# Layer 0 of a streaming encoder trunk on one core: half B's x^T through the staging pool, dense GLA products ahead of the decay products, the cache set-up queued at step 8, half B's recurrences written behind the projection

## The chip, the cores and the metric

The kernel runs on one core of a Trainium2 chip. The metric is the device time of one execution in microseconds (us), lower is better. Four compute engines work side by side, each through its own instructions in order: PE (TensorE, matmuls), DVE (VectorE), ACT (ScalarE) and POOL (GpSimd). SP (SyncE) issues nearly all DMAs, also in order; an instruction that waits on it holds up every DMA issue behind it.

## The reference, cut to what matters

Two layers over 1024 prompt frames and 64 sample frames, all float32. Layer 0 is the one that the change touches:

```python
p   = x @ w_in_mix                       # 1024 -> 3344 columns, for every frame
ya  = rwkv7_time_mix(p[..., :1792])      # mixer A: 8 heads x 64, a recurrence over time
yb  = gla_mix(p[..., 1792:])             # mixer B: 4 heads, key 64, value 128, chunked recurrence
#     q, k, v, xa, rg = split(p[..., 1792:])
#     log_a = log_sigmoid(xa @ alpha_up + alpha_bias) / 16     (the decay)
mix = concat([ya, yb]) @ w_out_mix
x   = layer_norm(alpha * x + mix)
x   = layer_norm(alpha * x + swiglu(x, w_ffn_in, w_ffn_out))
```

Layer 1 replaces the two mixers by chunk-band softmax attention, in which sample frames also read a cache of 128 earlier K and V rows per head.

## The kernel before, in words

The frames are cut into half A (384 prompt frames and the 64 sample frames, 448 columns) and half B (640 prompt frames). Every large product is done to float32 accuracy with three matmuls: each operand is split into a rounded high part and a low part (`wh`/`wl` for weights, `xh`/`xl` for x^T), and high*high, high*low and low*high are summed in one PSUM bank. `load_w` (L93) brings a 512 KB weight piece into `wr` (two buffers), casts it on ACT (L100) and takes the difference on DVE (L105) or POOL (L107); `wh` and `wl` have four buffers each. `load_xt` (L207) does the same for x^T: a DMA into a raw tile (L213), the cast to `xh` on ACT (L214), the difference `xl` on DVE or POOL (L215). Without a pool its raw tile is one of the two `wr` buffers; with the pool `yp` it is one of eight `yr` buffers. `gemm_ws` (L115, rows L123 to L125) and `gemm_ts` (L127, rows L134 to L137) are the dense products, with three PSUM banks `gps` in turn.

Half B's x^T has storage of its own for three of its eight pieces (`xeh`, `xel`); the other five lie in the storage of half A's x^T (`xt_tiles_in`, L195). The mixers' results of half A are later brought into that storage as well (`load_xt(0, self.yg_d, ...)`, from the DRAM tensor `yg_d`).

Order of layer 0 as written in `run` (L1331): input products of half A for mixer A (`inproj_rwkv`), the first four steps of its recurrences, then those for mixer B (`inproj_gla`, L338), then the rest of half A's recurrences (`rwkv`, `gla`); half B's x^T, `inproj_gla(1)` and `inproj_rwkv(1)`; half A's mixer results into x^T; `self.PRE` = 4 steps of half B's recurrences; the output projection of half A with its layer norm (`proj`, L853, wname `w_om`); the other recurrence steps of half B; the feed-forward of half A (`ffn`), whose 22 steps carry side work: at step 6 `bias_setup`, at step 8 `cache_setup` (L1111). `inproj_gla` computes first the decay (the narrow products L351 into 32 rows, the float32 products L362, then activations on DVE, ACT and POOL), then q and k (four weight pieces through `gemm_ws`), then v (L134 to L137), then the gate.

One recurrence step of mixer A is a unit that passes through `rw1` (loads rkv, xg, rsb; matmuls L436 to L438), `rw1b` (L483, L508 to L510), `rw2` (L576 to L583 and a chain of small DVE operations, L548 and L550), `rw3` (L610 to L621) and `rw4` (L648, the result goes to `yg_d` at L653). Mixer B's unit is `gla_unit` (L724 to L755, result at L759). Their matmuls are small, 64 or 128 columns each.

`cache_setup` handles four groups of V rows one after another: load `cv` (L1116, one buffer), cast to `cvh` on ACT (L112), difference on DVE (L113), write to DRAM (L1119); then two groups of K rows (L1122 to L1130).

The written order is not the order on the engines. A scheduler that runs while the kernel is built gives each engine its order: of the instructions that its own model of time has ready, the one written first goes first; a waiting one lets later ones by. So side work can be placed far ahead of where it is written. On the chip each engine then keeps that order whatever the real times are. `tc.issue_after(i)` puts every instruction that its block writes for the engine of `i` behind `i` on that engine; `last_w` is the latest weight DMA on SP.

Of the kernel before, what the change touches and what calls it, by code (L numbers as in the profile page):

```python
# [9 lines left out]
F32 = mybir.dt.float32  # L10
# [9 lines left out]
NA, NB = PA + 64, 1024 - PA  # L20
NM = max(NA, NB)
# [61 lines left out]
class Kern:  # L83
# [9 lines left out]
    def load_w(self, src, shape):  # L93

        nc = self.nc
        raw = self.wp.tile(shape, F32, tag="wr", name="wr", bufs=2)
        self.last_w = nc.sync.dma_start(raw, src).ins
        hi = self.wp.tile(shape, F32R, tag="wh", name="wh", bufs=self.WB)
        lo = self.wp.tile(shape, F32R, tag="wl", name="wl", bufs=self.WB)
        self.A.copy(hi, raw)  # L100
        self.wcount += 1
        m = shape[1]
        h = m * 5 // 8 if self.both else m * (self.wcount % 2)
        if h:
            self.V.tensor_tensor(lo[:, :h], raw[:, :h], hi[:, :h].bitcast(F32), op=ALU.subtract)  # L105
        if h < m:
            self.G.tensor_tensor(lo[:, h:], raw[:, h:], hi[:, h:].bitcast(F32), op=ALU.subtract)  # L107
        return hi, lo
# [229 lines left out]
    def inproj_gla(self, hf, pool):  # L338
        nc, V, A, G, T = self.nc, self.V, self.A, self.G, self.T
        n, c0, xt = self.N[hf], self.base[hf], self.xt[hf]  # L340

        raw = pool.tile([128, 8, 16], F32, tag="xar", name="xar", bufs=1)
        nc.sync.dma_start(raw, self.a["w_xa"])
        whl = pool.tile([128, 8, 32], F32R, tag="xaw", name="xaw", bufs=1)
        A.copy(whl[:, :, 0:16], raw)
        V.tensor_tensor(whl[:, :, 16:32], raw, whl[:, :, 0:16].bitcast(F32), op=ALU.subtract)
        segs = self.banks(hf)
        for kt in range(8):
            for i, xx in enumerate((xt.h(kt), xt.l(kt))):
                for ps, s0, w in segs:  # L350
                    T.matmul(ps[0:32, :], whl[:, kt, :], xx[:, s0 : s0 + w], start=(kt + i == 0), stop=(kt + i == 8))  # L351
        xa = pool.tile([32, NM], F32, tag="xa", name="xa", bufs=1)
        for ps, s0, w in segs:
            V.tensor_copy(xa[:, s0 : s0 + w], ps[0:32, :])
        up = pool.tile([32, 256], F32, tag="up", name="up", bufs=1)
        nc.sync.dma_start(up, self.a["up2"])
        for p in range(2):
            segs = self.banks(hf)
            mn = pool.tile([128, NM], F32, tag="sq", name="mn", bufs=3)[:, :n]
            ab = pool.tile([128, NM], F32, tag="sq", name="abz", bufs=3)[:, :n]  # L360
            for ps, s0, w in segs:
                T.matmul(ps, up[:, 128 * p : 128 * p + 128], xa[:, s0 : s0 + w], start=True, stop=True)  # L362
                V.tensor_scalar(mn[:, s0 : s0 + w], ps, self.ab[:, p : p + 1], 0.0, op0=ALU.add, op1=ALU.min)
                A.activation(ab[:, s0 : s0 + w], ps, AF.Abs, bias=self.ab[:, p : p + 1])
            A.activation(ab, ab, AF.Exp, scale=-1.0)
            A.activation(ab, ab, AF.Ln, bias=self.one)
            G.tensor_tensor(ab, ab, mn, op=ALU.subtract)
            nc.sync.dma_start(self.qkl_d[2, p, :, c0 : c0 + n], ab)
        for ct in range(4):
            w = self.load_w(self.a["w_in"][14 + ct], [128, 8, 128])  # L370
            segs = self.banks(hf)
            self.gemm_ws(w, xt, segs)
            t = pool.tile([128, NM], F32, tag="t1", name="gq", bufs=2)
            for ps, s0, wd in segs:
                A.copy(t[:, s0 : s0 + wd], ps)
            nc.sync.dma_start(self.qkl_d[ct // 2, ct % 2, :, c0 : c0 + n], t[:, :n])
        ws = []
        for i in range(4):
            hi, lo = self.load_w(self.a["w_gv"][i], [128, 2, 512])
            ws += [(hi[:, 0, :], lo[:, 0, :]), (hi[:, 1, :], lo[:, 1, :])]  # L380
        for i0 in range(0, n, 128):
            m = min(128, n - i0)
            ps = self.bank()[:m]
            self.gemm_ts(ps, ws, xt.h, xt.l, list(range(8)), lambda x: x[:, i0 : i0 + m])
            t = pool.tile([128, 512], F32, tag="xs", name="gvs", bufs=2)
            A.copy(t[:m], ps)
            nc.sync.dma_start(self.gv_d[c0 + i0 : c0 + i0 + m, :], t[:m])
        for ct in range(4):
            w = self.load_w(self.a["w_in"][18 + ct], [128, 8, 128])
            segs = self.banks(hf)  # L390
            self.gemm_ws(w, xt, segs)
            t = pool.tile([128, NM], F32, tag="t1", name="grg", bufs=2)
            for ps, s0, wd in segs:
                A.activation(t[:, s0 : s0 + wd], ps, AF.Tanh, scale=0.5)
                V.scalar_tensor_tensor(t[:, s0 : s0 + wd], t[:, s0 : s0 + wd], 1.0, ps, op0=ALU.add, op1=ALU.mult)
            nc.sync.dma_start(self.sg_d[ct, :, c0 : c0 + n], t[:, :n])
# [934 lines left out]
    def run(self):  # L1331
        nc, tc, a = self.nc, self.tc, self.a
# [2 lines left out]
        self.gla_d = self.dp.tile([2, 128, 128], F32, name="gla_d", tag="gla_d")  # L1335
        self.JX = 6
        self.PB, self.QB, self.turn, self.AQ = 1, 2, 0, (1, 4)
        self.HB, self.PRE, self.JO, self.JM = 5, 4, 16, 18
        es_scan, es_one, es_ps = ExitStack(), ExitStack(), ExitStack()
        self.sp_ps = es_ps.enter_context(tc.tile_pool(name="scps", bufs=1, space=PS))  # L1340
        self.tpsum = lambda: self.sbank("tps")
# [3 lines left out]
        yp = es_yr.enter_context(tc.tile_pool(name="yr", bufs=1))  # L1345
# [16 lines left out]
        for _ in g:  # L1362
            pass
        self.xt[1] = self.xt_tiles_in(es_one.enter_context(tc.tile_pool(name="xb", bufs=1, side="right")), 8 - NA * 8 // NB)
        self.load_xt(1)
        self.inproj_gla(1, one)
        self.inproj_rwkv(1, one)
        nc.sync.dma_start(a["s_shift"].rearrange("c p -> p c"), self.shS)
# [27 lines left out]
        for j in self.ffn(0, 0, acc0, hp, lambda: self.layer_norm(0, acc0, "ln2", 0, xd(0))):  # L1396
            if j == 6:
                self.bias_setup(hp)
            if 12 <= j < 20:
                for h in range(2 * j - 24, 2 * j - 22):  # L1400
                    self.bias_copies(h)
            if j == 8:
                with tc.tile_pool(name="as", bufs=1) as asp:
                    self.cache_setup(asp)
        for p in range(4):
            self.wkv_out(sc, S[p], a["p_wkv"][2 * p : 2 * p + 2])
# [173 lines left out]
```

## Time and profile before

| | us |
|---|---|
| Median of 3 runs (lowest to highest) | 3120.83 (3118.74 to 3125.66) |
| Profiled execution, its own time | 3122.28 |
| its span, first to last instruction | 3120.5 |
| PE busy in the span | 3010.1 |
| DVE / POOL / ACT busy | 2018.0 / 1347.8 / 1263.3 |
| mean granted PE clock | 0.977 |

"Busy" is the time in which at least one instruction of the engine ran. The granted clock is the share of TensorE's full rate; in stretches it is one half. A line of the timeline reads: start, length, engine, line, operation, output <- inputs, and in brackets the engine's idle time just before it with what ended that. A line of the stage table reads: from:to, length, then busy time (and instructions) of PE, PEld (weight loads), DVE, ACT, POOL, then granted clock, the DMA engines' busy share and GB/s. A line of the waits reads: who waited for whom, total us, times, longest.

### The profile page before, as it was taken

To read this page: it belongs to the slowest core of one execution; us is meant where nothing else is said; L and a number is where in the kernel's file an instruction comes from. 1 tells how busy PE (TensorE), PEld (TensorE's weight loads), DVE (VectorE), ACT (ScalarE), POOL (GpSimd) and SP (SyncE) were. 2 spreads that over 40 slices of the span, in tenths; PEclk is the share of its full clock that TensorE was granted. 3 is DMA by queue.
4 is the path that set the end of the run, shared out by engine and by line. 5 is a ranking of instruction groups with operands and counts; after the bars stand their busy time and mean duration, and the time that the engine had idled before them with its cause. 6 is when DMAs were issued, how large, how long until landed. Compare 5 with 4: busy or idle time off the path is not lost. (4 is left out here: it accounts for less than half of the span.)

```text
span 3120.5 us, 50008 instructions
## 1 busy us (share of the span) xinstructions
PE 3010.1 (96%) x17468; PEld 2675.3 (86%) x17468; DVE 2018.0 (65%) x4933; ACT 1263.3 (40%) x2753; POOL 1347.8 (43%) x1481
## 2 busy tenths in 40 slices
PE   8999999799999999999999999999999989899998
PEld 7888888688888887888999899899999978799987
DVE  5677875779898764375554466244666657866567
ACT  4454554344454323334442132354444433333332
POOL 2354533445455333343342233244555445754444
PEclk9989999889999999999999999999999999999999
DMA  6554434533533228534342222766445532322222
GB/s 200 141 154 120 108 111 122 141 109 107 145 106 110 85 100 277 180 98 122 116 130 97 81 95 99 240 192 190 126 139 141 150 130 82 116 84 95 63 86 75
DMA packets 297340, 395.10 MB, mean 127 GB/s; under 512 B 125376, under 2 KB 218424, under 8 KB 297088
## 3 DMA queue, kind: packets, MB, share of 16 engines
q1 hardware_dynamic: 295936, 389.28, 41.8%
q8 instruction: 138, 2.26, 0.3%
q10 hardware_dynamic: 1152, 2.62, 0.2%
q14 instruction: 114, 0.93, 0.1%
HBM read 319.44 MB, written 75.51 MB: 127 GB/s over the span
## 5 line engine op out<-in xcount | busy, mean ns | idle before, releaser
L107 POOL TENSOR_TENSOR wl<-wr,wh 128x512 fp32r<-128x512 f32 (+2 forms) x289 | 506.2, 1756 | 629.5 <-ACT wh L100 590.0
L123 PE MATMUL gps<-xh,wh 128*128 128x320 f32 (+1 forms) x2188 | 747.8, 342 | 9.0 <-ACT xh L214 5.9
L124 PE MATMUL gps<-xl,wh 128*128 128x320 f32 (+1 forms) x2188 | 746.5, 341 | 0.6 <-DVE xl L215 0.6
L125 PE MATMUL gps<-xh,wl 128*128 128x320 f32 (+1 forms) x2188 | 744.0, 340 | 0.7 <-DVE wl L105 0.6
L100 ACT CAST wh<-wr 128x1024 fp32r<-128x1024 f32 x352 | 366.9, 1048 | 468.2 <-PE gps L124 147.0
L105 DVE TENSOR_TENSOR wl<-wr,wh 128x512 fp32r<-128x512 f32 (+2 forms) x289 | 284.0, 983 | 255.1 <-ACT wh L100 253.2
L123 PEld LDWEIGHTS gps<-xh,wh 128*128 128x128 f32 x2188 | 415.5, 190 | 30.6 <-ACT xh L214 5.9
L125 PEld LDWEIGHTS gps<-xh,wl 128*128 128x128 f32 x2188 | 414.6, 189 | 19.5 <-DVE wl L105 1.8
L124 PEld LDWEIGHTS gps<-xl,wh 128*128 128x128 f32 x2188 | 414.8, 190 | 18.4 <-DVE xl L215 1.0
L1288 POOL TENSOR_SCALAR s<-s,mx 128x640 f32<-128x640 f32 (+5 forms) x144 | 203.6, 1414 | 289.6 <-DVE mx L1287 250.6
L134 PE MATMUL gps<-wh,xh 128*128 128x512 f32 x661 | 261.3, 400 | 11.5 <-ACT xh L214 7.1
L135 PE MATMUL gps<-wl,xh 128*128 128x512 f32 x661 | 261.5, 398 | 1.1 <-DVE wl L105 0.8
L137 PE MATMUL gps<-wh,xl 128*128 128x512 f32 x661 | 257.3, 397 | 4.8 <-DVE xl L215 4.8
L134 PE MATMUL gps<-wh,hh 128*128 128x512 f32 x572 | 225.9, 397 | 0.4 <-DVE acc L825 0.3
L135 PE MATMUL gps<-wl,hh 128*128 128x512 f32 x572 | 226.0, 396 | 0.0
L825 DVE TENSOR_TENSOR acc<-acc,gps 128x512 f32<-128x512 f32 (+1 forms) x216 | 143.7, 679 | 86.0 <-PE gps L137 80.7
L137 PE MATMUL gps<-wh,hl 128*128 128x512 f32 x484 | 189.8, 397 | 2.9 <-DVE hl L936 2.9
L548 DVE TENSOR_TENSOR t<-lt,x 16x48 f32<-16x48 f32 (+9 forms) x540 | 147.6, 273 | 39.9 <-DMA lt<-l_d 29.4
L1286 ACT ACTIVATE s<-s,mx 128x640 f32<-128x640 f32 (+5 forms) x144 | 96.5, 670 | 178.6 <-DVE mx L1285 172.1
L134 PEld LDWEIGHTS gps<-wh,xh 128*128 128x128 f32 x661 | 125.3, 190 | 40.9 <-ACT xh L214 7.3
L137 PEld LDWEIGHTS gps<-wh,xl 128*128 128x128 f32 x661 | 124.7, 189 | 32.4 <-DVE xl L215 5.3
L550 DVE TENSOR_TENSOR x<-x,t 16x48 f32<-16x48 f32 (+9 forms) x540 | 144.0, 267 | 10.9
(355 smaller groups left out, 6307.4 us busy)
## 6 DMA issues: line engine op xcount, KB each, us to landing
wr<-in_w_fi SPq DMA_DIRECT2D x176, 512.0 KB
wr<-in_w_fo SPq DMA_DIRECT2D x88, 512.0 KB
wr<-in_w_in SPq DMA_DIRECT2D x44, 512.0 KB
wr<-in_w_qk SPq DMA_DIRECT2D x32, 512.0 KB
qs<-qd SPq DMA_DIRECT2D x32, 320.0 KB
wr<-in_w_om SPq DMA_DIRECT2D x16, 512.0 KB
wr<-in_w_v SPq DMA_DIRECT2D x16, 512.0 KB
vd<-vh SPq DMA_DIRECT2D x16, 512.0 KB
```

What stands on the lines that cost most here:

```text
L100: self.A.copy(hi, raw)
L105: self.V.tensor_tensor(lo[:, :h], raw[:, :h], hi[:, :h].bitcast(F32), op=ALU.subtract)
L107: self.G.tensor_tensor(lo[:, h:], raw[:, h:], hi[:, h:].bitcast(F32), op=ALU.subtract)
L123: self.T.matmul(ps, hi[:, kt, :], xh, start=(kt == 0), stop=False)
L124: self.T.matmul(ps, hi[:, kt, :], xl, start=False, stop=False)
L125: self.T.matmul(ps, lo[:, kt, :], xh, start=False, stop=(kt == nk - 1))
L134: self.T.matmul(ps, xh, wh, start=(i == 0), stop=False)
L135: self.T.matmul(ps, xh, wl, start=False, stop=(lo is None and i == n - 1))
L137: self.T.matmul(ps, cols(lo(kt)), wh, start=False, stop=(i == n - 1))
L548: V.tensor_tensor(tv, lt[:, j, w:16].unsqueeze(2).to_broadcast([m, r, w]), x[:, 0, j, 0:w].unsqueeze(1).to_broadcast([m, r, w]), op=ALU.mult)
L550: V.tensor_tensor(x[:, 0, w:16, 0:w], x[:, 0, w:16, 0:w], tv, op=ALU.add)
L1288: G.tensor_scalar(s[:m, :nk], s[:m, :nk], mx[:m, 3:4], None, op0=ALU.mult)
```

## The change

Four edits, all in layer 0; no product and no element-wise operation is added or dropped.

1. Half B's x^T comes through the eight `yr` buffers instead of the two `wr` buffers, and each piece in two halves of 320 columns: sixteen loads, casts and differences instead of eight of 640 columns.
2. In `inproj_gla` the q and k products stand ahead of the decay products, for both halves.
3. `cache_setup` is written inside two `issue_after` blocks: its DMAs stand behind the latest weight DMA on SP, its ACT operations behind the latest weight cast on ACT. For that `load_w` keeps the cast as `last_cast`.
4. `self.PRE` is 0 instead of 4: no step of half B's recurrences is written ahead of the projection of half A.

```diff
@@ load_w
-        self.A.copy(hi, raw)
+        self.last_cast = self.A.copy(hi, raw).ins
@@ inproj_gla, ahead of the decay products
+        for ct in range(4):
+            w = self.load_w(self.a["w_in"][14 + ct], [128, 8, 128])
+            segs = self.banks(hf)
+            self.gemm_ws(w, xt, segs)
+            t = pool.tile([128, NM], F32, tag="t1", name="gq", bufs=2)
+            for ps, s0, wd in segs:
+                A.copy(t[:, s0 : s0 + wd], ps)
+            nc.sync.dma_start(self.qkl_d[ct // 2, ct % 2, :, c0 : c0 + n], t[:, :n])
@@ inproj_gla, behind the decay products: the same eight lines
-        for ct in range(4):
...
@@ run
-        self.HB, self.PRE, self.JO, self.JM = 5, 4, 16, 18
+        self.HB, self.PRE, self.JO, self.JM = 5, 0, 16, 18
@@ run
-        self.load_xt(1)
+        for kt in range(8):
+            for c in (0, NB // 2):
+                self.load_xt(1, None, (kt,), slice(c, c + NB // 2), yp)
@@ run, step 8 of the feed-forward of half A
-                with tc.tile_pool(name="as", bufs=1) as asp:
+                with tc.tile_pool(name="as", bufs=1) as asp, tc.issue_after(self.last_w), tc.issue_after(self.last_cast):
                     self.cache_setup(asp)
```

What the scheduler makes of it, at three places. In the changed file the lines from L341 on shift (the decay's L351 is L359, L362 is L370, L1369 is L1371).

PE, where half A's last dense product ends. Before, small products of half A's recurrences follow and then half B's decay products (`xaw` holds their weights; `xeh` and `xel` are half B's own x^T pieces):

```order
L125 MATMUL gps<-xh_69,wl 128x448
L436 MATMUL pa<-xg,w2z 128x128
L437 MATMUL pa<-xg,a2z 128x128
L438 MATMUL pa<-xg,g_209 128x128
L576 MATMUL pz<-tt,lab 128x64
L610 MATMUL ps<-sv,ro 64x64
L648 MATMUL py<-ident,on 128x64
L351 MATMUL gps<-xeh,xaw 32x320 x2
L351 MATMUL gps<-xel,xaw 32x320 x2
```

Now the same place goes on with half B's first dense product:

```order
L438 MATMUL pa<-xg,g_209 128x128
L576 MATMUL pz<-tt,lab 128x64
L614 MATMUL ps<-rr,btt 64x64 x2
L648 MATMUL py<-ident,on 128x64
L123 MATMUL gps<-xeh,wh 128x320
L124 MATMUL gps<-xel,wh 128x320
L125 MATMUL gps<-xeh,wl 128x320
```

The decay products of half B moved behind four dense weight pieces; there, ahead of half B's v products, they again stand in one block with small products and no dense one.

SP, where half B's last input product ends (`rkv_d` is its result in DRAM, `acc` the accumulator of the projection, `gb` the layer norm's weights, `yraw` a piece of half A's mixer results). Before, with loads of the cache (`cv`), of half B's first recurrence units (`rkv`) and the last `yg_d` write and `yraw` load behind them:

```order
L1116 DMA cv<-in_ck_v 128x4x64
L302 DMA rkv_d<-xs 128x640
L1369 DMA out_dram<-shP 128x14x1
L97 DMA wr<-in_w_om 128x1024
L426 DMA rkv<-rkv_d 128x3x128
L653 DMA yg_d<-y 128x128
L1119 DMA vd<-cvh 128x512
L1116 DMA cv<-in_ck_v 128x4x64
L213 DMA yraw<-yg_d 128x448
```

Now, the last `yg_d` write and the last `yraw` load standing further ahead and no cache load near:

```order
L302 DMA rkv_d<-xs 128x640
L1371 DMA out_dram<-shP 128x14x1
L866 DMA gb<-in_ln_w 128x1024
L866 DMA gb<-in_ln_b 128x1024
L796 DMA acc<-in_x 128x1024 x3
L796 DMA acc<-in_x 64x1024
L426 DMA rkv<-rkv_d 128x3x128 x2
```

The loads of `acc` and `gb` moved ahead of the load of half B's first units.

ACT, at the cache's V rows (`cvh`). Before, at the start of the projection of half A, between operations of the recurrences and ahead of the cast of a `yraw` piece:

```order
L112 CAST cvh<-cv 128x4x64
L612 COPY rr<-ps 64x128
L753 ACTIVATE gon<-gon,grstd 128x128
L112 CAST cvh<-cv 128x4x64
L440 ACTIVATE th<-pa,w0h 128x128
L442 ACTIVATE tha<-pa,a0h 128x128
L444 COPY gt<-pa 128x128
L214 CAST xh_69<-yraw 128x448
```

Now, in the feed-forward of half A, behind two weight casts:

```order
L100 CAST wh<-wr 128x1024 x2
L112 CAST cvh<-cv 128x4x64
L615 ACTIVATE uv<-ps 64x128
L716 ACTIVATE genb<-gb 128x64
L732 COPY gkt<-gpa 128x128
L493 COPY ro<-ar 64x2x128 x2
L629 COPY on<-ps 128x128
L501 COPY ec<-eb 64x2 x2
L746 COPY gon<-gps 128x128
L714 ACTIVATE geb<-gb 128x64
L112 CAST cvh<-cv 128x4x64
```

The four casts moved some 300 operations back on ACT and stand eight or more operations apart there.

More of the change, by code (lines that the diff above doesn't have):

```diff
@@ L368, in inproj_gla @@
             nc.sync.dma_start(self.qkl_d[2, p, :, c0 : c0 + n], ab)
-        for ct in range(4):
[L370 to L376, printed above, removed]
         ws = []
```

## The prediction

> **What bounds the kernel now.** I read the page first, then the stage table, then the waits, then the timelines of the stages that stood out. From the page:
>
> ```profile
> span 3120.5 us, 50008 instructions
> PE 3010.1 (96%) x17468; PEld 2675.3 (86%) x17468; DVE 2018.0 (65%) x4933; ACT 1263.3 (40%) x2753; POOL 1347.8 (43%) x1481
> ```
>
> PE is busy for 3010.1 of 3120.5 us and the change takes no matmul away. So it can win only two things: PE's idle time, 110 us in all, and the time in which PE is busy at half clock. The stage table, cut where the change acts, shows where these lie:
>
> ```profile
> 169.00:203.00 34.00, 31.65 (x153) 23.96 (x152) 25.39 (x71) 19.96 (x54) 19.84 (x36) 0.65 0.50 148
> 203.00:534.00 331.00, 325.12 (x2317) 290.06 (x2316) 252.91 (x906) 165.87 (x494) 141.08 (x264) 0.99 0.42 120
> 534.00:567.00 33.00, 18.09 (x79) 14.52 (x77) 18.78 (x65) 11.42 (x35) 11.02 (x17) 0.70 0.66 136
> 567.00:611.00 44.00, 42.37 (x220) 34.52 (x219) 39.00 (x98) 14.88 (x39) 21.27 (x26) 0.99 0.51 142
> 611.00:646.00 35.00, 27.94 (x141) 22.19 (x140) 30.68 (x80) 16.24 (x47) 23.53 (x30) 0.62 0.37 114
> 646.00:1014.00 368.00, 363.69 (x2296) 313.30 (x2295) 321.50 (x1058) 171.77 (x516) 179.87 (x290) 0.99 0.42 115
> ```
>
> Three short stages have a low clock: the passage from half A's to half B's input products (169 to 203, clock 0.65), the start of half A's output projection (534 to 567, 14.9 us idle, clock 0.70) and its layer norm (611 to 646, clock 0.62). Everything else up to 1014 us runs at 0.99. What PE waited for from 470 to 650 us:
>
> ```profile
> PE pb L483 <- ACT gt L444: 8.5, 1, 8.5
> PE gps L137 <- DVE xl L215: 4.8, 1, 4.8
> PE pz L581 <- ACT ys L579: 4.4, 1, 4.4
> ```
>
> The longest is named after an ACT copy, but ACT's timeline shows who held ACT, and SP's who held that:
>
> ```profile
> 545.88 0.40 ACT L753 ACTIVATE gon<-gon,grstd 128x128 f32<-128x128 f32 x1
> 558.62 0.40 ACT L112 CAST cvh<-cv 128x256 fp32r<-128x256 f32 x1 [12.33 <-DMA cv<-in_ck_v]
> 559.43 0.26 ACT L444 COPY gt<-pa 128x128 f32<-128x128 f32 x1
> 560.20 0.56 ACT L214 CAST xh<-yraw 128x448 fp32r<-128x448 f32 x1 [0.50 <-DMA yraw<-yg_d]
> ```
> ```profile
> 542.18 0.51 SPq L302 DMA_DIRECT2D rkv_d<-xs  x1
> 543.27 1.37 SPq L97 DMA_DIRECT2D wr<-in_w_om  x1
> 552.67 0.36 SPq L426 DMA_DIRECT2D rkv<-rkv_d  x1
> 553.12 0.44 SPq L653 DMA_DIRECT2D yg_d<-y  x1
> 554.12 0.39 SPq L1116 DMA_DIRECT2D cv<-in_ck_v  x1
> 557.57 0.32 SPq L213 DMA_DIRECT2D yraw<-yg_d  x1
> 561.45 1.82 SPq L796 DMA_DIRECT2D acc<-in_x  x4
> ```
>
> SP stood from 544.6 to 552.7 before the load of a half-B unit (L426). Behind it queued the last result of half A (L653), the cache load (L1116) and the last x^T piece (L213). ACT then stood 12.33 us before the cast of that cache load, with `gt` and everything of the projection behind it. So two pieces of work that the projection doesn't need, the cache set-up and half B's first units, hold it up. What SP waited for is in its own list:
>
> ```profile
> SPq L426 <- DMA rkv_d<-xs: 9.2, 2, 8.0
> ```
>
> **Edit by edit.** The sum is made against the profiled execution, 3122.28 us (span 3120.5, 1.8 us around it); it lies 1.45 us above the median of the runs, 3120.83.
>
> *Edits 3 and 4 at the projection.* Two marks in PE's timeline:
>
> ```profile
> 534.39 0.50 PE L134 MATMUL gps<-wh,xh 128*128 128x512 f32 x1
> 559.75 2.08 PE L483 MATMUL pb<-ar,bbk 128*128 128x128 f32 x8 [8.51 <-ACT gt L444]
> 567.06 0.80 PE L134 MATMUL gps<-wh,xpk 128*128 128x512 f32 x1
> ```
>
> Between the first and the third, 32.7 us, PE did 36 dense matmuls; at full pace they follow each other every 0.23 us:
>
> ```profile
> 574.84 0.39 PE L134 MATMUL gps<-wh,xh 128*128 128x512 f32 x1
> 575.06 0.39 PE L135 MATMUL gps<-wl,xh 128*128 128x512 f32 x1
> ```
>
> That is 8.3 us; the small products that now stand among them take about 4 us more, and the first two differences of x^T 1 to 2 us: some 14 us at best. But the row at 567.06 needs a fourth PSUM bank, so the first accumulation on DVE must be done, and that needs `acc`. In the new order the `acc` loads stand behind the `rkv_d` write and, I assume, wait for it to land, since `acc` takes over storage of the input products. From the rows: the write is issued 8 us after the dense work ended (542.18 against 534.39) and lands 10.5 us later (552.6) at most; without the cache's traffic beside it I take 5. From the issue of `acc` to the accumulation,
>
> ```profile
> 565.73 0.67 DVE L823 SCALAR_TENSOR_TENSOR acc<-acc,gps 128x512 f32<-128x512 f32 x1
> ```
>
> 4.3 us pass (561.45 to 565.73), to which the `gb` loads ahead add perhaps 3. So the third mark comes at 8 + 5 + 4.3 + 3 = 20 us, between 14 and 26, instead of 32.7: **-12 us (-19 to -6)**. The wait on `acc` is what is late next. The late `yg_d` write is no longer: it stands ahead of the last two input products' writes.
>
> *The rest of the projection and its layer norm*, 567 to 646. DVE is busy for 39.00 of 44 and 30.68 of 35 us there, nearly the bound. With edits 3 and 4 fewer recurrence and cache operations stand among the projection's on DVE (79 rows against 99 by the order, from half B's last input product to the first layer-norm operation; 73 against 85 inside the norm), which at 0.4 us each could give 8 to 13 us back. Against it, some ten more small products of the recurrences stand in PE's queue between the last dense product and the feed-forward, where the clock is 0.62; eight such matmuls took 2.08 us at 559.75, so ten items of two to four are 5 to 10 us. I take **-4 us (-10 to +5)**.
>
> *Edits 1 and 2 at the passage to half B.*
>
> ```profile
> 170.47 0.47 PE L351 MATMUL gps<-xeh,xaw 128*32 128x320 f32 x2
> 177.44 0.48 PE L351 MATMUL gps<-xl,xaw 128*32 128x320 f32 x2 [0.96 <-DVE xl L215]
> 198.31 0.64 PE L123 MATMUL gps<-xeh,wh 128*128 128x320 f32 x1
> ```
>
> For 28 us no dense product runs. The granted share of 0.65 over 34 us is 11.9 us lost to the clock, though PE hardly idles, and 2.4 us are idle: 14 us at stake. Edit 2 puts dense products right behind half A's. Edit 1 has most raw data in `yr` by then, so only casts and differences remain. They cannot start before half A's last products, since five of the eight pieces lie in half A's storage. POOL takes 0.8 us for a half piece (half of the row below), six in a row, while PE's first piece needs one every six matmuls of 320 columns, 0.9 us by the 0.23 us for 512: a stall of 0 to 3 us.
>
> ```profile
> 167.33 1.56 POOL L215 TENSOR_TENSOR xl<-xraw,xh 128x640 fp32r<-128x640 f32 x1 [3.98 <-ACT xh L214]
> ```
>
> The block of decay products isn't dissolved, it comes later, with some 14 small items among it instead of 26. If it loses as this one does, in proportion, that is about 8 us, plus 2 for the new passage: **-4 us (-11 to +2)**.
>
> Here the Trainium skill bears. "TensorE: Matmul & The Clock Gate", section "What's actually happening", says that the clock halves after an idle window of about 3.4 us and is full again after one busy window. By that, neither this block nor the layer norm's tail should stay at half clock while filled. The table disagrees: 31.65 of 34 us busy at 0.65, 27.94 of 35 at 0.62. Small products alone did not keep the clock up here, and the sum goes by the table.
>
> *Edit 1 at the start.* Sixteen issues on SP instead of eight, at 0.32 to 0.51 us by SP's rows above: 8 x 0.4 = 3.2 us more of SP, and 2.6 MB moved into half A's products, ahead of weight loads that run with buffers to spare. Hidden there by dense work; I take **+1 us (-1 to +4)**. The Trainium skill's "DMA: Bandwidth & Descriptors", "Rules for kernel authors", speaks against halving: it asks for transfers of 1 MiB or more and for coalescing. No run here shows this load's rate either way.
>
> *Edit 3 at step 8.* The four casts now queue in ACT in the feed-forward, each behind a DMA on SP, and weight casts, PSUM evacuations and recurrences queue behind them. What ACT and PE waited for from 646 us on:
>
> ```profile
> ACT btt L565 <- DMA t<-t_d: 19.9, 11, 5.5
> PE gps L137 <- DVE hl L936: 2.9, 2, 1.7
> PE tps L895 <- DVE xl L113: 2.6, 1, 2.6
> ```
>
> ACT stands before such DMAs up to 5.5 us at a time there already, and PE's two largest sums of waits up to 1170 us are 2.9 and 2.6 us. Four more of 2 to 5 us each are covered by the weights in four buffers; if that cover is gone, each costs what it exceeds. **+1 us (0 to +12)**.
>
> *All else in the new order.* From 203 to 534 and 646 to 1014 PE idles 5.9 and 4.3 us; the order there is new throughout and will have waits of its own: **+1 us (-4 to +7)**.
>
> Sum: -12 - 4 - 4 + 1 + 1 + 1 = -17 us, so 3122.3 - 17 = 3105 us.
>
> **The rivals.** *The wait moves to `acc` (no change).* If the `rkv_d` write takes its 10.5 us and `gb` delays `acc` by 4 more, the third mark is at 26 us; DVE, standing before `acc`, has the recurrences behind it and gives back nothing, and the block of decay products costs as much as before: -6 + 2 = -4, 3118 us. For it: DVE at 88% in the stage. Against it: the cache's traffic is gone from the queues.
>
> *Slower: the cache set-up stalls the feed-forward.* The 12.33 us on ACT came from SP standing before another wait, and at step 8 SP also has recurrence loads between the `cv` loads. One such stall cost PE 8.5 us and some 3 of the 9.9 us that the clock took in that stage (0.30 of 33). The first cast has its load well ahead; three could repeat it, 3 x 12 = 36 us at about 12 each, and with -17 that is +19: 3141 us. Two give +7. It decides from two stalls over 10 us on; against it, ACT's waits there end within 5.5 us.
>
> *More than forecast.* By the rule of the clock gate above, filled stretches run at full clock: of the 13.3 us that the layer norm loses to its clock and the 11.9 of the passage, the 12 that the sum leaves lost would go too: 3105 - 12 = 3093 us. The table speaks against it.
>
> *An edit does not act.* The scheduler places by readiness, so PRE = 0 need not move half B: the first L648 of half B stands at about the same place on PE in both orders. Then only the cache's stall goes: the last `yg_d` write would still stand 8 us on SP. About -9 us, 3113.
>
> **How the numbers follow.** Forecast (gain of 8 to 25 us) 0.50; the wait moves to `acc` 0.20; stalls at step 8, or other waits of the new order, slower 0.14; full clock 0.06; an edit does not act 0.10. A measurement of this kernel can tell about 0.2%, 6.2 us. Faster: 0.50 + 0.06 + 0.09 of the last = 0.65; same: 0.20 + 0.01 = 0.21; slower 0.14. The range leaves out the full-clock case below and most of the slower case above: 3090 to 3126.
>
> **What would show it.** Right: no `cvh` cast before 700 us; the mark of the first `xpk` matmul 15 to 25 us behind the projection's first, with DVE's wait before it named `acc`; a clock above 0.85 in that stage; a first half-B dense matmul within 5 us of half A's last. Wrong: that mark after 30 us; ACT waits over 10 us at `cvh` in the feed-forward with PE idle beside them; a layer norm longer than 40 us from the last dense product to the feed-forward; new PE waits over 5 us between 200 and 530 us.

## The result and the profile after

The changed kernel takes 3151.09 us (median of 4 runs, 3149.59 to 3151.56), the kernel before 3122.41 beside it: ratio 1.0093, 95% interval 1.008 to 1.0106. It is 29 us slower, where 17 us faster was forecast. From the page of the profile after:

```profile
span 3149.6 us, 50092 instructions
PE 3030.0 (96%) x17468; PEld 2685.2 (85%) x17468; DVE 2003.8 (64%) x4937; ACT 1264.1 (40%) x2761; POOL 1345.3 (43%) x1485
```

PE has the same 17468 matmuls, is busy 19.9 us longer and idles 9.2 us longer. To see where, both programs are cut at the same work, counted in PE's dense products (rows L123 to L137): after the 600th (half A's input products are nearly done), the 1000th (half B's q, k and decay are done), the 1800th (half A's projection starts), the 2000th (feed-forward), the 3400th, the 3600th (entry to the attention stage) and the 3800th. The stage table of before:

```profile
5.90:164.20 158.30, 152.42 (x719) 128.28 (x720) 95.86 (x296) 73.64 (x139) 51.82 (x58) 0.97 0.58 167
164.20:304.50 140.30, 136.33 (x833) 116.43 (x833) 106.86 (x343) 73.05 (x205) 65.69 (x114) 0.91 0.46 136
304.50:534.40 229.90, 225.64 (x1664) 202.43 (x1662) 172.29 (x635) 115.34 (x348) 97.17 (x186) 0.99 0.42 117
534.40:650.10 115.70, 92.10 (x452) 74.64 (x450) 90.78 (x253) 42.91 (x121) 57.15 (x76) 0.79 0.49 126
650.10:1132.40 482.30, 477.99 (x2949) 410.09 (x2948) 395.38 (x1229) 213.09 (x604) 216.57 (x330) 1.00 0.39 110
...
1192.60:1237.70 45.10, 44.42 (x205) 37.56 (x204) 21.32 (x27) 20.15 (x28) 20.04 (x14) 1.00 0.88 298
```

and the same stages of the changed kernel:

```profile
6.00:177.30 171.30, 158.06 (x722) 130.13 (x723) 95.11 (x299) 76.05 (x149) 54.52 (x60) 0.94 0.59 172
177.30:316.30 139.00, 138.57 (x902) 118.69 (x901) 106.32 (x391) 77.45 (x227) 74.33 (x134) 0.96 0.41 120
316.30:553.50 237.20, 225.07 (x1594) 200.03 (x1594) 169.75 (x622) 114.71 (x335) 91.55 (x173) 0.96 0.40 112
553.50:665.70 112.20, 96.64 (x463) 77.93 (x463) 87.45 (x239) 33.74 (x88) 44.25 (x59) 0.76 0.43 106
665.70:1155.20 489.50, 484.28 (x2935) 413.24 (x2934) 388.91 (x1211) 216.35 (x626) 220.97 (x343) 0.99 0.40 113
...
1215.50:1268.60 53.10, 46.80 (x204) 38.67 (x203) 22.17 (x28) 20.84 (x30) 24.18 (x18) 0.94 0.85 276
```

Stage by stage the change costs +13.0, -1.3, +7.3, -3.5 and +7.2 us, then +0.1 in the stage left out, +8.0 at the entry to the attention stage and -1.8 in all the rest: 29 us. The projection with its layer norm, for which 16 of the 17 us were forecast, gives 3.5. The loss sits at places for which the prediction had no term, or only the +1 of "all else": half A's input products, half B's behind the decay block, the feed-forward, and the entry to the attention stage, some 150 us behind the cache's last write (1063 us). A good part of it is PE's clock, the third figure from the end of each row: it falls in five of the six stages, and one minus it, times the stage's length and summed over the six rows, is 60 us against 44. Idle time has its share too: in the third stage PE idles 12.1 us (237.2 less 225.07) instead of 4.3.

The start of the projection in the changed kernel, on PE, DVE and SP (three answers of the timeline):

```profile
553.51 0.77 PE L134 MATMUL gps<-wh,xh 128*128 128x512 f32 x1
...
578.66 0.77 PE L134 MATMUL gps<-wh,xpk 128*128 128x512 f32 x1 [7.19 <-DVE x L550]
```
```profile
577.76 0.69 DVE L823 SCALAR_TENSOR_TENSOR acc<-acc,gps 128x512 f32<-128x512 f32 x1 [10.29 <-DMA acc<-in_x]
```
```profile
558.89 0.33 SPq L302 DMA_DIRECT2D rkv_d<-xs  x1
559.27 0.43 SPq L1371 DMA_DIRECT2D out_dram<-shP  x1
...
561.74 0.63 SPq L866 DMA_DIRECT2D gb<-in_ln_b  x1
572.28 1.87 SPq L796 DMA_DIRECT2D acc<-in_x  x4
```

The first `xpk` product comes 25.2 us behind the first product, and DVE waits 10.29 us for `acc`, as forecast. `acc` is late because SP stands from 562.4 to 572.28 for the `rkv_d` write to land: 13.4 us from its issue, where the prediction took 5. Between the two stands a row that the prediction passed over, in before as well: the output of the shift vectors.

### The profile page after: what moved, and what is told of

Read it like the earlier page. It is cut to its first block, busy times and chain, and to the rows that moved or that the text cites. A ratio compares the mean times of both kernels' runs of the same rounds, so it can differ in the third digit from the quotient of the medians.

```text
span 3149.6 us, 50092 instructions
## 1 busy us (share of the span) xinstructions
PE 3030.0 (96%) x17468; PEld 2685.2 (85%) x17468; DVE 2003.8 (64%) x4937; ACT 1264.1 (40%) x2761; POOL 1345.3 (43%) x1485
## 5 line engine op out<-in xcount | busy, mean ns | idle before, releaser
L123 PE MATMUL gps<-xh,wh 128*128 128x320 f32 (+1 forms) x2188 | 750.3, 343 | 12.5 <-ACT wh L100 6.5
L100 ACT CAST wh<-wr 128x1024 fp32r<-128x1024 f32 x352 | 367.0, 1048 | 482.8 <-PE gps L124 159.5
L123 PEld LDWEIGHTS gps<-xh,wh 128*128 128x128 f32 x2188 | 416.5, 190 | 35.0 <-ACT wh L100 8.1
L137 PE MATMUL gps<-wh,xl 128*128 128x512 f32 x661 | 258.2, 398 | 0.2 <-DVE xl L215 0.2
L137 PE MATMUL gps<-wh,hl 128*128 128x512 f32 x484 | 188.3, 395 | 0.0
L135 PEld LDWEIGHTS gps<-wl,xh 128*128 128x128 f32 x661 | 127.1, 192 | 32.3 <-DVE wl L105 4.1
L137 PEld LDWEIGHTS gps<-wh,xl 128*128 128x128 f32 x661 | 125.0, 189 | 28.5 <-DVE xl L215 0.9
```

What stands on the lines that cost most here:

```text
L100: self.last_cast = self.A.copy(hi, raw).ins
L123: self.T.matmul(ps, hi[:, kt, :], xh, start=(kt == 0), stop=False)
L135: self.T.matmul(ps, xh, wl, start=False, stop=(lo is None and i == n - 1))
L137: self.T.matmul(ps, cols(lo(kt)), wh, start=False, stop=(i == n - 1))
```

## The experiments

All ratios are against runs of before on the same chip, in brackets the 95% interval. Before's medians there are 3118.7 to 3121.0 us; beside the changed kernel it was 3122.4. So where a run is compared with the changed kernel, the excess of each over its own before is what counts: 28.7 us for the changed kernel.

### Each edit alone

The first question was which edit loses. The diff of each is its part of the change, on before.

*Edit 1 alone.* 

> Before with edit 1 alone (half B's x^T through the staging pool, in column halves). Theory 1, the decay products: the 19 us that the changed kernel has lost when it reaches half A's output projection come from edit 2, so this run lies within 5 us of before (ratio 0.9984 to 1.0016) and its passage to half B is shorter than before's 34 us. Theory 2, x^T: sixteen loads, casts and differences queued among half A's input products delay these; then this run alone is 10 to 20 us slower (1.003 to 1.006), lost between 100 and 180 us.

Measured: 3128.09 us, ratio 1.0025 (1.0014 to 1.0036).

*Edit 2 alone.* 

> Before with edit 2 alone (decay products behind the q and k products, both halves). Theory 1, the decay products: half A's decay block now stands where PE has only small products beside it, it stalls PE and halves its clock, and the recurrences that need its result bunch up behind it: 10 to 20 us slower (1.003 to 1.006), and half A's projection starts at 544 to 554 us instead of 534. Theory 2, x^T: within 5 us of before (0.9984 to 1.0016).

Measured: 3143.15 us, ratio 1.0071 (1.0056 to 1.0086).

*Edit 3 alone.* 

> Before with edit 3 alone (cache set-up held back to step 8). Theory A: it does what the prediction said, the stall of 8.5 us before pb and its clock loss go and nothing new comes in the feed-forward: 5 to 14 us faster (0.9955 to 0.9984). Theory B: the gain is given back in the feed-forward and behind it, where the set-up now shares ACT and SP with the recurrences: within 5 us of before (0.9984 to 1.0016).

Measured: 3131.66 us, ratio 1.0034 (1.0023 to 1.0045).

*Edit 4 alone.* 

> Before with edit 4 alone (PRE 4 to 0). Theory A: the recurrences of half B come later, in a feed-forward where DVE is already busy 321 of 368 us; their longer chain delays the feed-forward and wkv_out: 5 to 12 us slower (1.0016 to 1.004). Theory B: the projection and its layer norm gain what the feed-forward loses: within 5 us of before (0.9984 to 1.0016).

Measured: 3142.18 us, ratio 1.0068 (1.0054 to 1.0082).

Every edit alone loses, about 7, 22, 11 and 21 us: twice the loss of all four together. So the losses are not sums of separate prices. And none lies in a range set for it: edit 1 falls between its two theories, edits 2 and 4 lose more than any foresaw, and edit 3 was to win or cost nothing. Edit 3 was to remove a stall of 8.5 us; this is PE's longest wait between 525 and 700 us in its trace, and after it that of edit 4 alone:

```profile
PE pt L508 <- DVE t L548: 10.3, 1, 10.3
```
```profile
PE pb L483 <- POOL lw L450: 10.5, 1, 10.5
```

The stall is there without the cache set-up, and it is there without the early units. Neither by itself was its cause. And in three of the four traces (edits 1, 3 and 4) the stage from the 3600th to the 3800th dense product takes 51 to 53 us instead of 45.1, as in the changed kernel.

### What holds up the projection: one small output

The bytes that the DMA queues moved answer the first. In before, over 8 us behind the shift output, and in 10 us behind the other shift output (94 to 104 us, issued at 91.61 by L1368):

```profile
DMA packets 1081, 0.38 MB, mean 47 GB/s; under 512 B 986, under 2 KB 986, under 8 KB 1081
```
```profile
DMA packets 71, 0.29 MB, mean 29 GB/s; under 512 B 1, under 2 KB 1, under 8 KB 71
```

The queues are taken, 77.4% of 16 engines' time in the second stretch, and move almost nothing. Packet by packet: each output is written as 1792 elements of 4 bytes (14 x 128, transposed by the access pattern), sent within 2 us (805 of the first line's 986 small packets are the tail of that write); then for 8 to 10 us over half of the packets of 4096 bytes take more than 1 us each, the longest 5.8 and 10.4, where 0.16 is usual. A crawl of this length comes twice in the whole program, behind these two writes. The test changes nothing but the access pattern, the order on every engine stays word for word:

```diff
-nc.sync.dma_start(a["p_shift"].rearrange("c p -> p c"), self.shP)
+nc.sync.dma_start(a["p_shift"].rearrange("c p -> (c p)").rearrange("(p c) -> p c", c=14), self.shP)
```

and the same for `s_shift`. It leaves out the transposition of the two outputs, so it is a test and no version to use.

*On before.* 

> Before with the two shift outputs (L1368, L1369) written in 128 runs of 56 bytes instead of 1792 single elements; every engine's order stays as it was. It leaves out the transposition of these two small outputs. Theory S, the scattered write: behind each of the two writes all DMA traffic crawls for about 10 us (packets of 4096 bytes at 1 to 4.6 us instead of 0.16), and the second of them, not the cache set-up or the rkv_d write, holds up the start of half A's projection: the rkv_d write lands in under 4 us instead of 10.5, PE's wait of 8.5 us before pb goes, the first xpk matmul stands 18 to 26 us behind the projection's first instead of 32.7, and the run is 8 to 16 us faster (ratio 0.995 to 0.9975). Rival, queues full of weights, cache and recurrence traffic as such: within 4 us of before (0.9987 to 1.0013) and the wait stays.

Measured: 3110.29 us, ratio 0.9975 (0.9964 to 0.9985), 9.4 us faster by the medians and 7.8 by the ratio, at the low end of the range. The 10 us from 94 us on and 8 us behind the second write now read

```profile
DMA packets 1245, 1.06 MB, mean 106 GB/s; under 512 B 686, under 2 KB 1116, under 8 KB 1244
```
```profile
DMA packets 1735, 1.53 MB, mean 191 GB/s; under 512 B 795, under 2 KB 1441, under 8 KB 1735
```

and the wait before `pb` falls from 8.51 to 0.98 us; the first `xpk` product stands at 559.17, 25.9 us behind the projection's first instead of 32.7:

```profile
551.45 1.16 PE L483 MATMUL pb<-ar,bbk 128*128 128x128 f32 x8 [0.98 <-ACT gt L444]
559.17 0.76 PE L134 MATMUL gps<-wh,xpk 128*128 128x512 f32 x1 [0.96 <-POOL bk L467]
```

The cache set-up and the units of half B are still there. The rival is out: the crawl is the scattered write's, and so is the stall. The wait for `rkv_d` is 4.3 us from its issue, a little more than the 4 expected.

*On the changed kernel.* 

> The changed kernel with the same two writes in runs of 56 bytes; its order otherwise unchanged, and the transposition of the two outputs left out. Theory S: PE's wait of 7.19 us before the first xpk matmul goes, that matmul comes 13 to 19 us behind the projection's first instead of 25.2, as the prediction's sum had it, and the run is 7 to 14 us faster than the changed kernel, 3137 to 3144 us (1.005 to 1.0075 against before). Rival: 3147 to 3155 us (1.008 to 1.0105).

Measured: 3134.58 us, ratio 1.0047 (1.003 to 1.0065), 16.5 us faster than the changed kernel by the medians, 14 by the excess over before. The `xpk` mark is 18.5 us behind the first product (562.79 against 544.3), as the prediction's sum had it, and SP now gets past the `rkv_d` write 3.9 us behind its issue, where the changed kernel took 13.4:

```profile
550.01 0.33 SPq L302 DMA_DIRECT2D rkv_d<-xs  x1
...
553.93 2.13 SPq L796 DMA_DIRECT2D acc<-in_x  x4
```

Two thirds of the gain are elsewhere: the 600th dense product comes at 166.5 us instead of 177.3. There the changed kernel shows, on ACT and on PE:

```profile
108.81 1.04 ACT L100 CAST wh<-wr 128x1024 fp32r<-128x1024 f32 x1 [9.12 <-DMA wr<-in_w_gv]
```
```profile
113.72 0.69 PE L610 MATMUL ps<-sv,ro 128*64 128x64 f32 x4 [2.79 <-ACT sv L516]
...
126.83 0.50 PE L134 MATMUL gps<-wh,xh 128*128 128x512 f32 x1
```

The first shift output is written when half A's mixer-A products end. In the changed kernel the q and k products come next, so that when the crawl holds back the first v weights, their cast stands in ACT with the evacuations of q and k and the recurrences' copies behind it, and PE has only decay products and small ones: no dense product from 108.8 to 126.8 us, 18.1 us against 7.3 with harmless writes.

### The entry to the attention stage

ACT's order there in before, then in the changed kernel, with PE's row:

```profile
1211.70 1.44 ACT L214 CAST xh<-yraw 128x640 fp32r<-128x640 f32 x2 [2.03 <-DMA yraw<-yg_d]
1213.05 1.05 ACT L100 CAST wh<-wr 128x1024 fp32r<-128x1024 f32 x1
1214.64 0.72 ACT L214 CAST xh<-yraw 128x640 fp32r<-128x640 f32 x1 [0.54 <-DMA yraw<-yg_d]
1215.27 1.04 ACT L100 CAST wh<-wr 128x1024 fp32r<-128x1024 f32 x1
```
```profile
1239.71 0.72 ACT L214 CAST xh<-yraw 128x640 fp32r<-128x640 f32 x1 [0.65 <-DMA yraw<-yg_d]
1240.70 1.52 ACT L214 CAST xh<-yraw 128x640 fp32r<-128x640 f32 x2 [0.27 <-DMA yraw<-yg_d]
1242.13 1.99 ACT L100 CAST wh<-wr 128x1024 fp32r<-128x1024 f32 x2
```
```profile
1243.22 0.74 PE L123 MATMUL gps<-xh,wh 128*128 128x448 f32 x1 [4.42 <-ACT wh L100]
```

In before the first weight cast stands behind two casts of half B's next x^T; in the changed kernel behind five (three of them in these rows). These x^T pieces are not needed before the next output projection. No edit touches this place; that the scheduler's choice there follows from what was shifted ahead of it is the likely reason, not shown. The test holds the loads back:

```diff
-with tc.tile_pool(name="yr1", ...) as yp:
+with tc.tile_pool(name="yr1", ...) as yp, tc.issue_after(self.last_w), tc.issue_after(self.last_cast):
     self.load_xt(1, self.yg_d, (4, 5, 6, 7, 0, 1, 2, 3), pool=yp)
```

> The changed kernel with half B's x^T loads of the attention stage (L1424 and the following) queued behind the weights traced before them. Theory Q, ACT's queue at the first q and k product: in the changed kernel three x^T casts stand ahead of the two weight casts there, PE waits 4.4 us, and the stage around 1220 to 1245 us takes 8 us more than before; with the loads behind, this goes: 6 to 10 us faster than the changed kernel, 3141 to 3145 us (ratio 1.0065 to 1.008). Rival, the PE work there is only displaced or the loads cost as much further on: within 4 us of the changed kernel (1.008 to 1.0105).

Measured: 3139.13 us, ratio 1.0067 (1.0055 to 1.0079). Its excess over before is 20.5 us instead of 28.7, so the queue cost 8 us, and the trace has these 8 us at this place: the stage takes 45.0 us (1211.4 to 1256.4) instead of 53.1. (The bare medians differ by 12, but before's differ by 4.)

*Both causes taken away.* 

> The changed kernel with the x^T loads of the attention stage queued behind the weights and the two shift outputs in runs of 56 bytes; it leaves out the transposition of these two outputs. If the two causes are separate, their gains add: 16 us from the writes, 6 to 10 from the queue, 3125 to 3129 us (ratio 1.0015 to 1.003). If they overlap: above 3131 us.

Measured: 3122.65 us, ratio 1.0016 (1.0007 to 1.0024). The excess over before is 4 to 5 us, so 24 of the 28.7 us are gone where the single gains were 14 and 8: they add, within what such runs can tell.

*The same ground without the edits.* 

> Before with neither disturbance: the shift outputs in runs of 56 bytes (their transposition left out) and the x^T loads of the attention stage queued behind the weights. PE's order is before's but for the attention stage, and before has no wait at its first q and k product, so this should be the run with 56-byte runs again: 3107 to 3113 us (ratio 0.996 to 0.998). If the queueing gains by itself, below 3104 us.

Measured: 3107.35 us, ratio 0.9965 (0.9952 to 0.9978). So on equal ground, with neither disturbance in either kernel, the four edits still cost 15 us.

### What the edits cost by themselves

*Without edit 2.* 

> The changed kernel without edit 2 (decay products ahead of q and k again). Theory 1, the decay products carry most of the loss: 15 to 25 us of the 29 go, ratio 1.0015 to 1.0045. Rival, the other three together lose as much as they do apart (7, 11 and 21 us): ratio 1.007 to 1.0125.

Measured: 3134.82 us, ratio 1.0049 (1.0034 to 1.0064). The excess over before is 15 us, so about 14 of the 28.7 go: half of the loss, just under the 15 that Theory 1 asked for at least, and far from the rival.

*Edit 2 on the ground.* 

> The ground with edit 2 alone. Theory S, the later decay products leave the weights' wait behind the scattered write uncovered: of the 22 us that edit 2 costs on before, 10 to 14 go, 8 to 12 us above the ground. Rival, the decay block and the recurrences behind it cost the time by themselves: 18 us or more above the ground.

Measured: 3125.0 us, ratio 1.002 (1.0011 to 1.0029), 17.6 us above the ground, just under the rival's 18. Theory S fails here: the two disturbances explain some 4 of edit 2's 22 us, and the later decay block with what stands behind it the rest. Which half?

*Half A only.* 

> The ground with edit 2 in half A alone. In the run with edit 2 in both halves the program stood 3.5 us behind the ground after half A's q and k products and passed to half B a little sooner. If half B's decay block is what costs: within 5 us of the ground, 3107.4 us (3102 to 3113). If half A's order is what costs, by delaying the recurrences that need its decay: 10 us or more above it.

Measured: 3113.31 us, ratio 0.9975 (0.9965 to 0.9986), 6 us above the ground by the medians and 3 by the ratios, at the edge of the smaller forecast.

*Half B only.* 

> The ground with edit 2 in half B alone. If half B's decay block is what costs, at half clock between 224 and 316 us and in the recurrences bunched behind it: 10 to 18 us above the ground (3117 to 3126). If half A's order is what costs: within 5 us of the ground.

Measured: 3123.22 us, ratio 1.0011 (1.0002 to 1.002), 15.9 us above. Most of it is half B's. (The two halves apart come to somewhat more than both together.) The first three stages of the ground, then of this run, cut at the same dense products:

```profile
5.90:159.50 153.60, 151.13 (x719) 126.71 (x720) 96.02 (x296) 73.69 (x139) 52.15 (x58) 0.99 0.55 172
159.50:300.80 141.30, 133.04 (x833) 113.40 (x833) 108.66 (x344) 73.20 (x205) 66.30 (x114) 0.95 0.46 136
300.80:531.90 231.10, 227.00 (x1663) 203.38 (x1661) 171.99 (x635) 115.63 (x348) 97.26 (x186) 0.99 0.41 117
```
```profile
5.80:158.30 152.50, 149.91 (x720) 125.47 (x721) 94.40 (x296) 73.62 (x139) 51.20 (x58) 1.00 0.56 172
158.30:311.40 153.10, 146.38 (x919) 124.97 (x918) 119.03 (x402) 80.20 (x231) 76.56 (x132) 0.92 0.45 131
311.40:542.50 231.10, 223.01 (x1600) 200.10 (x1598) 165.71 (x618) 113.27 (x341) 94.43 (x181) 0.97 0.41 116
```

At the projection this run is 10.6 us behind, with 24 more items (matmuls) done, some 4 us at the 0.15 us an item found below. Lost to the clock are 0.08 x 153.1 + 0.03 x 231.1 = 19 us against 1.5 + 7.1 + 2.3 = 11 on the ground, 8 us more; with the items that is the 10.6 and a little over. The passage to half B still has 17.4 us without a dense product (ground: 25.9), and 46 us later the decay block adds 16.5 more. These two profiled executions differ by 10 us in all, the medians by 16, so the account covers what the traces show and not the rest.

*Edit 4 on the ground.* 

> The ground with edit 4 alone. Theory Q with W: of the 21 us that edit 4 costs on before, 8 are ACT's queue in the attention stage and some 4 the wait behind the scattered write, the rest is the layer norm at half clock and the displaced small products: 6 to 12 us above the ground. If the displacement alone is the cost: 18 us or more. If both disturbances were all of it: within 4 us of the ground.

Measured: 3116.54 us, ratio 0.9998 (0.9986 to 1.001), 9.2 us above the ground. The projection with its layer norm and the first 200 dense products of the feed-forward, of the ground and of this run:

```profile
531.90:640.50 108.60, 91.61 (x452) 74.33 (x450) 93.97 (x253) 42.86 (x121) 56.25 (x76) 0.80 0.45 134
640.50:704.70 64.20, 62.97 (x369) 55.11 (x367) 51.07 (x169) 25.89 (x72) 24.46 (x33) 0.97 0.36 102
```
```profile
525.80:636.00 110.20, 87.85 (x408) 71.12 (x408) 91.54 (x239) 36.97 (x95) 42.21 (x61) 0.78 0.43 125
636.00:712.80 76.80, 73.96 (x452) 63.94 (x451) 60.33 (x203) 34.34 (x106) 33.57 (x52) 0.96 0.35 98
```

PE has 44 items fewer in the projection, which takes 1.6 us longer all the same, for PE idles 22.4 us there instead of 17.0: the items had stood in its waits. The first part of the feed-forward has 83 more and takes 12.6 us longer, 0.15 us an item, 1.6 us of it new idle time; PE has hardly a wait there to put them into.

*Edits 3 and 4 on the ground.* 

> Before with edits 3 and 4 together, the two shift outputs in runs of 56 bytes and the x^T loads of the attention stage queued behind the weights, so that neither known disturbance is in it; it leaves out the transposition of the two shift outputs. To be read against before with 56-byte runs, 3110.3 us. Theory P, the prediction's steps hold once the writes are harmless: the projection to the feed-forward's start gains 12 to 16 us and the feed-forward gives back 1 to 2: 3094 to 3099 us (ratio 0.992 to 0.9935). Theory W, work only moves: the recurrences' small products that stood in the projection's waits now stand in a feed-forward in which PE has no idle time, the projection's gain is given back there: 3106 to 3118 us (0.9955 to 0.9995).

Measured: 3116.32 us, ratio 0.9993 (0.9984 to 1.0002), 9 us above the ground. The expectation names the run with 56-byte runs as its base, 3110.3: 6 above that. Theory W holds, and Theory P is out: even on ground where no write crawls, moving this work out of the projection gains nothing.

### Versions meant to beat both

*Transposed on PE at the old place.* 

> Before with the two shift vectors transposed on PE (two small products, two copies on DVE) and written as 14 runs of 512 bytes; the output is complete. Theory S: the gain of the run with 56-byte runs, 8 to 16 us, less or more by what the new order of the small work brings, which in the four single edits was between 7 and 22 us to the bad: ratio 0.995 to 1.003. Rival: no gain to start with, ratio 1.001 to 1.007.

Measured: 3119.3 us, ratio 1.0002 (0.9988 to 1.0016). No crawl, but 6.8 us of new idle time on PE ahead of the projection and again the wait at the entry to the attention stage.

*Transposed behind the feed-forward, x^T held back.*

```diff
+for dst, src in ((a["s_shift"], self.shS), (a["p_shift"], self.shP)):
+    ps = self.sbank("pso")
+    self.T.transpose(ps[0:14, 0:128], src, self.ident)
+    t = sc.tile([128, 128], F32, tag="gS0", name="sht", bufs=2)
+    self.V.tensor_copy(t[0:14, :], ps[0:14, 0:128])
+    nc.sync.dma_start(dst, t[0:14, :])
```

> Before with the shift vectors transposed on PE and written as 14 runs of 512 bytes behind the feed-forward, where the other states are written, and the x^T loads of the attention stage queued behind the weights; the output is complete. Theory S with Q: no crawl of the DMA queues anywhere, no wait at the first q and k product: 3104 to 3114 us (ratio 0.995 to 0.998). If the new order of the small work costs as in the run with the transposition in place: 3116 to 3124 us (0.9985 to 1.0015).

Measured: 3114.3 us, ratio 0.9988 (0.9979 to 0.9996), between the two forecasts: about 4 us of the ground's 11.

*The same with edit 1.* 

> The kernel with transposed shift vectors behind the feed-forward and queued x^T loads (3114.3 us, ratio 0.9988 before), with edit 1 added; the output is complete. In the trace of edit 1 alone the program stood 3.8 us ahead of before at the start of the attention stage, and lost it in ACT's queue there. If that gain is real: 3108 to 3113 us (ratio 0.997 to 0.9985). If not: 3113 to 3118 us.

Measured: 3113.27 us, ratio 0.9987 (0.9977 to 0.9997). Edit 1 adds nothing that could be told. Both beat before by about 0.1%, less than the ground's 0.35%. What takes the difference was not tried; the new order of the small work is the likely reason.

## Why the prediction was wrong, step by step

**Projection start (-12).** Mechanism right, size off: the mark came after 25.2 us, a gain of 7.5 and not 12, with DVE's wait named `acc` as forecast. The step that failed is "without the cache's traffic beside it I take 5" for the landing of `rkv_d`: it took 13.4. The cache's traffic had not been what slowed it; the shift output was, shown by the runs in which only the access pattern of the shift outputs changed: in the changed kernel's order the landing then took 3.9 us, and the mark came after 18.5, inside the 14 to 26 forecast. The prediction's reading of the wait was wrong with it: "two pieces of work that the projection doesn't need" were queued in the same crawl, they did not make it. The rival "the wait moves to `acc`" came closest here, with its mark at 26 us, though it took the write's 10.5 us over from before and knew no reason for them. The clock in this stage was 0.70, not above 0.85 (row below).

**Rest of the projection and layer norm (-4, -10 to +5).** From the mark to the feed-forward 83.0 us before, 87.0 after: +4, inside the range with the other sign. DVE did have a little less to do (87.45 us against 90.78 from the projection's start to the feed-forward), but the tail of the norm ran at low clock, the second of these two rows of the changed kernel; the first is the projection's start:

```profile
553.50:578.70 25.20, 16.97 (x66) 13.34 (x65) 12.22 (x40) 3.05 (x10) 3.80 (x6) 0.70 0.72 143
630.00:666.00 36.00, 33.10 (x160) 26.97 (x161) 26.79 (x90) 13.18 (x43) 17.48 (x30) 0.57 0.29 85
```

So the rival of full clock in filled stretches failed too: 33.1 of 36 us busy, at 0.57.

**Passage to half B (-4).** -1.3. Half B's products do follow half A's at once, and the decay block "comes later", as the text said: the 29.4 us without a dense product became 16.1 us, at 227 us. What the text lacked is the next stage, where the recurrences stand behind the later block: +7.3, under "all else" below.

**Missing: half A.** The change moves the decay products of both halves, and the working priced half B's alone. Half A's stage lost 13.0 us. The first scattered write costs 10.8 us in the changed kernel by the mark of the 600th dense product, and in before 2 to 5 (164.2 us against 162.4 and 159.5 in the two runs without it). With harmless writes the changed order still costs 4 to 5 us there (166.5 against 162.4, and 164.6 against 159.5); the other 8 to 9 came through the write.

**x^T at the start and cache at step 8 (+1 each).** Right. The four `cvh` casts stand at 852 to 879 us and ACT's waits for their loads sum to 1.3 us. The rival "slower" foresaw stalls there and gave +19 us: right sign, wrong cause, so that it came near the measured loss is luck.

**"All else in the new order" (+1, -4 to +7).** This is the step that lost most: the next stage of half B +7.3, the feed-forward +7.2, the attention entry +8.0, in all 22.5 us. The term rested on PE's idle time in before's trace, and it ended at 1014 us. In half B's stage the new order does have waits of its own, 12.1 us idle instead of 4.3: 6.4 us stand in four waits for a load from DRAM that the recurrences need (`tt`, L576), where before has 0.4. They stay with harmless writes (6.2), and no single edit brings them in. In the feed-forward PE idles only 0.9 us more, but its clock is 0.99 instead of 1.00, which over 489.5 us is some 5 us, and low clock is no idle time. On the ground, items moved out of the projection's waits cost PE their time where it has no waits; in the changed kernel the projection has as many items as before (463 and 452), so this alone is not its feed-forward's loss. The attention entry turned on a choice among ACT's casts, which before's trace can't show and the new order does.

Left open: on the ground edit 2 costs 17.6 us and edits 3 and 4 cost 9, yet the four together 15; which of them cover each other, and why the waits for `tt` come with the four together, was not tried.

## What to carry to other kernels

Before moving work out of the way of a wait, ask what the whole DMA system did in that stretch: bytes moved against queues busy shows a crawl that no waiting instruction names. Work that sits in a busy engine's waits is free there, and where there is no wait it costs its time, so a move has to be priced at both ends and in every copy of the code that it touches. Where a scheduler sets the order, run each edit alone and look for the stages that move without being touched.

## What the runs showed of the hardware

Two outputs of 7 KB, written as 1792 elements of 4 bytes each, slowed all DMA traffic behind them for 8 to 10 us, to 29 and 47 GB/s, at a cost of 8 to 9 us in before and 14 to 16 in the changed kernel. The Trainium skill, "DMA: Bandwidth & Descriptors", "Rules for kernel authors", says that a strided last dimension becomes one descriptor per element and is better made contiguous; the trace agrees: the two writes go out as 3584 packets of 4 bytes, and as 256 of 56 bytes when the rows are contiguous.
